# A hybrid attention and experts trunk on one core: one first-fit room for weight tiles, a three-tile split queue, a router without GpSimd

## The chip, the core and the metric

The kernel runs on one core of one Trainium2 chip. The metric is the device time of one execution in microseconds (us). TensorE multiplies, VectorE and ScalarE do elementwise work, GpSimd little of it, and SyncE (SP in the profile) issues the transfers of the weights from HBM to on-chip memory. PE is TensorE, DVE VectorE, ACT ScalarE and POOL GpSimd.

## The reference, cut to what matters

Two layers over 256 tokens of width 1024. Each layer has a norm, four kinds of attention heads side by side, an output projection and a residual add; then a norm and a SwiGLU. The first layer's SwiGLU is dense. The second's picks two of eight experts for each token:

```python
logits = (t @ router).astype(jnp.float32)
top_val, top_idx = lax.top_k(logits, TOP_K)
gates = jax.nn.softmax(top_val, axis=-1)
for e in range(N_EXPERTS):
    out = out + combine[:, e:e+1] * swiglu(t, w_gate[e], w_up[e], w_down[e])
```

An expert has matrices gate and up of 1024 x 3584 and down of 3584 x 1024, in float32. Eight experts are 352 MB of the 430 MB that the kernel reads. A final norm ends it.

## The kernel before, in words

**Weights come as a stream of tiles ("units").** `Stream` holds one ordered list for the whole kernel. Each unit is loaded in float32 by one DMA from SP's queue (L162) into a stage place. ScalarE then makes `hi`, the float16 of 512 times the weight (L169), and VectorE makes `lo`, what `hi` leaves over (L172). TensorE multiplies `hi` with the high and the low float16 part of the activations and `lo` with the high part (L1157, L1158 and L1161 for gate and up, L1190 and L1192 for down). One unit in eight of gate and up (k = 7) is left unsplit and multiplied in float32 (L1151, a flag in the unit's tuple).

**An expert is done in two halves of 1792 hidden columns.** For half i the main loop runs `gate_up(i)` and then `down(i - 1)`; `closing` does the down of the last half. A half of gate and one of up are 8 units each of 128 x 1792 (896 KB), a half of down is 7 units of two row blocks by 1024 columns (1 MB). After up, VectorE multiplies silu(gate) with up (L1178), ScalarE takes the float16 of it (L1179) and VectorE the rest (L1180). The last half's down ends in a unit of four row blocks by 512 columns and two of two row blocks by 512.

**Places.** The pool `stgp` has 9 stage buffers of 8320 bytes of a partition and `cvtp` six of 4160 for `hi` and six for `lo`, whatever the unit's size. In the last layer three more stage places are lent from elsewhere (tags e0, e2, e3, at steps 5, 10 and 16 of the attention's loop) and a fourth (xn) behind the router. A stage place is free once `lo` is made, or for an unsplit unit once TensorE has used it, and the next unit is loaded into it at once; places of `hi` and `lo` are free when TensorE has used the unit.

**Order.** The order of each engine's instructions is the order of the program. `done()` is called behind each used unit; it splits on until `ahead` units are split beyond the used one: three at the start of the kernel, then one more at every second unit up to five, and six in the experts stage. So on ScalarE and VectorE the split of a unit some places ahead stands in front of the work on a result that TensorE has yet to make. The last nine units of the list (`brisk`) are split in two parts each.

**Router.** `Plain` takes the squares of the rows (ScalarE), multiplies the rows with the norm's gain on GpSimd (`part`, L440), turns the rows on TensorE (`turn`) and multiplies them with the router matrix (`logits`). `moe` then makes the scale y of each row (`rstd_of`), the two largest logits (`top`), the one-hot masks, and the scaled rows in float16 as hh and hl. `slots(e)` makes the one-hot matrix of the slots of expert e (L1070), `gather` collects its tokens by a product with it (L1082), `gather_last` the float32 part for k = 7 (L1095, L1097). ScalarE splits one unit at the end of attention (`top_up`) and one more before the first half.

**Side work.** Gathers of the next expert and the return of the last one (`turn_back`, L1213 to L1216; `scatter`, L1222 and L1224) lie in a queue `side`. One job is taken behind each of k = 5, 6, 7 of up and behind each unit of down until the queue is empty.

Of the kernel before, what the change touches and what calls it, by code (L numbers as in the profile page):

```python
# [41 lines left out]
NB = FH // P  # L42

# [26 lines left out]
def hybrid_trunk_kernel(ctx: ExitStack, tc: tile.TileContext, a: dict, out: bass.AP, dbg=None):  # L70
# [4 lines left out]
    stgp = ctx.enter_context(tc.tile_pool(name="stgp", bufs=N_STG))  # L75
    cvtp = ctx.enter_context(tc.tile_pool(name="cvtp", bufs=N_CVT))
# [30 lines left out]
    def expert_units(sets, tail=False):  # L107

        got = []
        seq = [(s, h) for s in sets for h in range(2)]  # L110
        for i in range(len(seq) + 1):
            if i < len(seq):
                (wg, wu, _), h = seq[i]
                for w in (wg, wu):
                    got += [(rows(w, k * P, 1, h * FH, FH), 1, FH, k == KD - 1) for k in range(KD)]
            if i > 0:
                (_, _, wd), h = seq[i - 1]
                ends = tail and i == len(seq)
                got += [(rows(wd, h * FH + r * P, 2, 0, D), 2, D, False) for r in range(0, NB - 4 if ends else NB, 2)]
                if ends:  # L120
                    r0 = h * FH + (NB - 4) * P
                    got += [(rows(wd, r0 + r * P, kt, c0, 512), kt, 512, False) for r, kt, c0 in ((0, 4, 0), (0, 2, 512), (2, 2, 512))]
        return got

    MLA_KT = (2, 2, 4)
    units = []
    for layer in range(DEPTH):
# [10 lines left out]
        if layer % 2 == 0:  # L138
            units += dense_units(a["dense_w_gate"][j], a["dense_w_up"][j], a["dense_w_down"][j])
        else:  # L140
            sets = [(a["moe_w_gate"][j, e], a["moe_w_up"][j, e], a["moe_w_down"][j, e]) for e in range(NE)]
            units += expert_units(sets, layer == DEPTH - 1)

    class Stream:


        def __init__(self, units, stage_tile, part_tiles, ahead):
            self.units, self.stage_tile, self.part_tiles = units, stage_tile, part_tiles
            self.loaded = self.split = self.low = self.used = 0
            self.stage, self.place, self.high, self.ready = {}, {}, {}, {}  # L150
# [3 lines left out]
            self.brisk = 0  # L154

        def load_next(self, place=None):
            u = self.loaded
            if u < len(self.units):
                src, kt, n, _ = self.units[u]
                stg = self.stage_tile(u, place)  # L160
                self.place[u] = place
                nc.sync.dma_start(stg[:, : kt * n].rearrange("p (k n) -> p k n", k=kt), src)  # L162
                self.stage[u] = stg
                self.loaded += 1
            elif place is None and self.last:
                self.last.pop()()
# [7 lines left out]
        def split_next(self):  # L174
# [7 lines left out]
            m = self.units[u][1] * self.units[u][2]  # L182
            self.high[u] = self.part_tiles[0](u)
            self.split += 1
            if u >= len(self.units) - self.brisk:
                self.low_until(u)
                lo = self.part_tiles[1](u)
# [8 lines left out]
        def top_up(self):  # L196

            if self.split < min(len(self.units), self.used + N_CVT) and not self.units[self.split][3]:
                u = self.split
                self.high[u] = self.part_tiles[0](u)  # L200
                self.high_part(u, slice(0, self.units[u][1] * self.units[u][2]))
                self.split += 1

        def low_until(self, end):
            while self.low < end:
                if self.units[self.low][3]:
                    self.ready[self.low] = (self.stage[self.low],)
                    self.low += 1
                    continue
                lo = self.part_tiles[1](self.low)  # L210
                self.low_part(self.low, lo, slice(0, self.units[self.low][1] * self.units[self.low][2]))
                self.low_done(lo)

        def low_done(self, lo):
            u = self.low
            _, kt, n, _ = self.units[u]
            self.stage.pop(u)
            self.ready[u] = tuple(z[:, : kt * n].rearrange("p (k n) -> p k n", k=kt) for z in (self.high.pop(u), lo))
            self.low += 1
            self.load_next(self.place.pop(u))  # L220

        def get(self, later=0):
            while self.split <= self.used + later:
                self.split_next()
# [3 lines left out]
        def done(self):  # L228
# [3 lines left out]
            if self.units[u][3]:  # L232
                self.stage.pop(u)
                self.load_next(self.place.pop(u))
# [6 lines left out]
        def go(self):  # L241
            while not self.held and self.split < min(len(self.units), self.used + self.ahead):
                self.split_next()
# [10 lines left out]
    parts = (  # L254
        lambda u: cvtp.tile([P, 2080], F16, tag="hi", name=f"hi{u}"),
        lambda u: cvtp.tile([P, 2080], F16, tag="lo", name=f"lo{u}"),
    )

    def stage_tile(u, place):
        if place:  # L260
            return (ext if place[0] == "e" else com).tile([P, 2048], F32, tag=place, name=f"stg{u}")
        return stgp.tile([P, 2080], F32, tag="stg", name=f"stg{u}")

    stream = [Stream(units, stage_tile, parts, N_CVT - 1)]
    stream[0].ahead = 3
    stream[0].brisk = 9

# [158 lines left out]
    class Plain:  # L426
# [9 lines left out]
        def part(self, t, n):  # L436
# [3 lines left out]
            ge.tensor_tensor(self.xg[:, t, c], x[:, t, c], self.gain[:, c], op=OP.mult)  # L440

        def turn(self, t, half):
# [5 lines left out]
            if half == 0:  # L448
# [49 lines left out]
    def attention(layer, act, feed, follow):  # L498
# [346 lines left out]
        for i in range(NHD + 3):  # L845
# [8 lines left out]
            if i == NHD + 1 and layer == DEPTH - 1:  # L854
                late["gain"] = act.tile([P, 3, 384], F32, tag="tt", name="gain").rearrange("p a s -> p (a s)")[:, :D]
# [40 lines left out]
        wo_job("B", 1, (1,))  # L896
        nxt.part(1, 1)
        nxt.turn(1, 0)
        stream[0].top_up()
# [111 lines left out]
    def moe(layer, act, feed, follow):  # L1011
# [10 lines left out]
        feed.turn(1, 1)  # L1022
        top(0)
        pw = bank("acc", "warm_m")
        keep_warm(3, pw, ident16, cm16)
        feed.logits(1)
        ss = com.tile([P, NT], F32, tag="ss", name="ss_m")
        ve.tensor_tensor(ss, feed.ss[:, 0], feed.ss[:, 1], op=OP.add)
        y = rstd_of(ss, D, "m", NT)
# [16 lines left out]
        ve.tensor_scalar(hh[:, 1, :], xgf[:, 1, :], y[:, 1:2], None, op0=OP.mult)  # L1046
        for t in range(NT):
            se.activation(xgf[:, t, :], xgf[:, t, :], AF.Copy, scale=y[:, t : t + 1])
# [40 lines left out]
        def gather_last(e):  # L1089

            pe = pes.pop(e)
            ps = bank("side", f"gr{e}")
# [9 lines left out]
        def gathers(e):  # L1102
            return [lambda i=i, half=half: gather(e, i, half) for i in range(2) for half in range(2)] + [lambda: gather_last(e)]
# [3 lines left out]
        for t in range(NT):  # L1107
            ve.tensor_tensor(hl[:, t, :], xgf[:, t, :], hh[:, t, :], op=OP.subtract)
        ve.tensor_tensor(g2[:, :, 1], m8[:, :, 1], m8[:, :, 0], op=OP.subtract)
        ve.tensor_tensor(g2[:, :, 1], g2[:, :, 1], y, op=OP.mult)  # L1110
        se.activation(g2[:, :, 1], g2[:, :, 1], AF.Exp)
        for job in gathers(0):
            job()
# [29 lines left out]
        def into(ps, k, e):  # L1143
# [4 lines left out]
            if len(w) == 1:  # L1148
                for j in range(NB):
                    b, c = divmod(j, PER)  # L1150
                    te.matmul(ps[b][:, c * C : (c + 1) * C], w[0][:, j * P : (j + 1) * P], xr, start=False, stop=ends and j + 1 == spans[b][1])  # L1151
# [11 lines left out]

        def gate_up(i, e, tag, side):
            ps = [bank("gate", f"m{tag}g{i}_{b}") for b in range(len(spans))]
            for k in range(KD):
                into(ps, k, e)
            for b, (j0, j1) in enumerate(spans):
                se.activation(sg[:, j0 * C : j1 * C], ps[b][:, : (j1 - j0) * C], AF.Silu, scale=1.0 / SW)
            ps = [bank("up", f"m{tag}u{i}_{b}") for b in range(len(spans))]  # L1170
            for k in range(KD):
                into(ps, k, e)
                if k > 4 and side:
                    side.popleft()()
            hi, lo = hTs[i % 2]
            for b, (j0, j1) in enumerate(spans):
# [3 lines left out]
                ve.tensor_tensor(lo[:, c], sg[:, c], hi[:, c], op=OP.subtract)  # L1180

        def back_by(acc, i, r, w, k, ds):

            L = tuple(z[:, r * C : (r + 1) * C] for z in hTs[i % 2])
            first, ends = i % 2 == 0 and r == 0, i % 2 == 1 and r == NB - 1
            for part in range(2):
                for q, d in enumerate(ds):
                    dst = acc[d // 4][:, d % 4 * C : (d % 4 + 1) * C]
                    W = w[part][:, k, q * P : (q + 1) * P]
                    te.matmul(dst, W, L[0], start=first and part == 0 and d % 4 == 0, stop=ends and part == 1 and d % 4 == 3)  # L1190
                    if part == 0:
                        te.matmul(dst, W, L[1], start=False, stop=False)  # L1192

        accs = {}

        def down(i, tag, side):
            if i % 2 == 0:
                accs[i // 2] = [bank("down", f"m{tag}y{i}_{n}") for n in range(2)]
            for r in range(0, NB, 2):
# [4 lines left out]
                if side:  # L1204
                    side.popleft()()
# [27 lines left out]
        def final_gain():  # L1233
            fin["g"] = stgp.tile([P, 2080], F32, tag="stg", name="final_gain")[:, :D]
            nc.sync.dma_start(fin["g"], spread(a["final_norm"], D))
# [167 lines left out]
```

## Time and profile before

| | |
|---|---|
| median of 3 runs | 1368.21 us (1367.33 to 1368.56) |
| profiled execution | 1368.37 us, its span 1366.6 us |
| busy in the span | PE 93%, PEld (weight loads of TensorE) 83%, DVE 79%, ACT 66%, POOL 2% |
| loads of gate and up | 256 of 896 KB, 17.9 and 17.4 us to landing (median) |
| loads of down | 111 of 1 MB, 19.2 us to landing, and 2 of 512 KB |
| HBM read | 430.41 MB |

Times inside the span count from its first instruction. The router lies at 480 to 495 us, the experts behind it. In a timeline row the first number is the start and the second the duration; x is the count of instructions merged in the row, and the bracket tells how long the engine had stood idle and what ended that. "DMA share" is the mean busy share of the sixteen DMA engines (a little over 1 when all are busy), the clock a share of TensorE's full one. A matmul's own duration is its latency; matmuls overlap.

### The profile page before, as it was taken

How to read it: one execution, taken by the hardware profiler on the slowest of the kernel's cores; microseconds unless marked ns; L12 is line 12 of the kernel's file. 1: busy time of each engine (PE TensorE's matmuls, PEld its weight loads, DVE VectorE, ACT ScalarE, POOL GpSimd, SP SyncE). 2: the span in 40 equal slices, each digit the busy share in tenths (PEclk: the TensorE clock that was granted, in tenths of full speed). 3: DMA queues.
4: the chain of work that ended last, by engine and by line, in shares of the span. 5: the costliest groups of instructions: out<-in, count | busy, mean ns of one | idle time of the engine just before them, and what ended most of it. 6: DMA issues, size and time to landing. Idle time of an engine off the chain costs nothing.

```text
span 1366.6 us, 43224 instructions
## 1 busy us (share of the span) xinstructions
PE 1277.3 (93%) x19680; PEld 1134.5 (83%) x19680; DVE 1079.5 (79%) x1032; ACT 898.2 (66%) x916; POOL 32.4 (2%) x51
## 2 busy tenths in 40 slices
PE   8999999999999998999999998998998998999885
PEld 5785877777587688999989988998998998999874
DVE  6655775666564587899998898898898998989976
ACT  6554654444544576788777678677777776877764
POOL 2300000000010010000000000000000000000000
PEclk9999999999999999999999999999999999999998
DMA  9953475646443459999999999999999999999991
GB/s 272 353 171 124 155 247 198 203 149 203 156 172 111 175 196 392 400 406 414 413 411 416 412 412 416 411 411 412 408 414 402 403 416 408 410 405 407 412 361 57
DMA packets 128799, 434.35 MB, mean 318 GB/s; under 512 B 11936, under 2 KB 59440, under 8 KB 128480
## 3 DMA queue, kind: packets, MB, share of 16 engines
q1 hardware_dynamic: 126640, 429.72, 81.4%
q8 instruction: 156, 2.56, 0.8%
q0 software_dynamic: 928, 1.78, 0.5%
q14 instruction: 35, 0.29, 0.1%
q10 hardware_dynamic: 1040, 0.00, 0.0%
HBM read 430.41 MB, written 1.06 MB: 316 GB/s over the span
## 4 chain that ended last, share of the span: by engine, by line
PE 23%; DMA 19%; DVE 11%; issue 5%; ACT 3%; SPq 0%; DVEq 0%; ACTq 0%
DMA stg<-in_moe_w_down_dram 13%; DVE lo L172 8%; PE my L1190 5%; DMA stg<-in_moe_w_up_dram 3%; DMA stg<-in_moe_w_gate_dram 3%; PE mu L1151 2%; PE my L1192 2%; PE mg L1161 2%; PE mg L1158 2%; PE mg L1157 2%; PE mg L1151 1%; ACT hi L169 1%; PE mu L1158 1%; PE mu L1157 1%; PE mu L1161 1%
## 5 line engine op out<-in xcount | busy, mean ns | idle before, releaser
L172 DVE SCALAR_TENSOR_TENSOR lo<-stg,hi 128x1792 f16<-128x1792 f32 (+3 forms) x418 | 849.4, 2078 | 44.0 <-ACT hi L169 43.8
L169 ACT ACTIVATE hi<-stg 128x1792 f16<-128x1792 f32 (+3 forms) x418 | 714.4, 1738 | 154.0 <-DMA stg<-in_moe_w_down_dram 56.7
L1158 PEld LDWEIGHTS <-hi 128*128 128x128 f16 x3136 | 271.8, 98 | 11.3 <-issue 11.1
L1157 PEld LDWEIGHTS <-hi 128*128 128x128 f16 x3136 | 272.7, 99 | 4.2 <-issue 4.0
L1192 PE MATMUL my<-rest,hi 128*128 128x96 f16 x1792 | 182.9, 208 | 0.9 <-issue 0.9
L1190 PE MATMUL my<-rest,hi 128*128 128x96 f16 x1792 | 183.0, 208 | 0.3 <-issue 0.3
L1190 PEld LDWEIGHTS <-hi 128*128 128x128 f16 x1792 | 157.6, 99 | 6.2 <-issue 3.3
L1192 PEld LDWEIGHTS <-hi 128*128 128x128 f16 x1792 | 157.2, 99 | 4.1 <-issue 1.0
L1157 PE MATMUL mg<-xgh,hi 128*128 128x96 f16 x1568 | 151.3, 208 | 8.0 <-DVE x L1224 6.0
L1158 PE MATMUL mg<-xgl,hi 128*128 128x96 f16 x1568 | 151.5, 208 | 5.4 <-issue 5.3
L1161 PEld LDWEIGHTS <-lo 128*128 128x128 f16 x3136 | 146.3, 98 | 5.2 <-issue 3.5
L1157 PE MATMUL mu<-xgh,hi 128*128 128x96 f16 x1568 | 147.1, 206 | 0.1
L1158 PE MATMUL mu<-xgl,hi 128*128 128x96 f16 x1568 | 147.1, 206 | 0.0
L1190 PE MATMUL my<-rest,lo 128*128 128x96 f16 x1792 | 115.4, 208 | 7.9 <-DVE lo L172 7.2
L1190 PEld LDWEIGHTS <-lo 128*128 128x128 f16 x1792 | 89.6, 99 | 9.6 <-DVE lo L172 8.6
L1161 PE MATMUL mg<-xgh,lo 128*128 128x96 f16 x1568 | 86.7, 207 | 2.9 <-issue 2.9
L1161 PE MATMUL mu<-xgh,lo 128*128 128x96 f16 x1568 | 85.2, 206 | 0.1
L459 PEld LDWEIGHTS <-hi 128*128 128x128 f16 x640 | 62.6, 98 | 9.9 <-issue 2.7
L460 PEld LDWEIGHTS <-hi 128*128 128x128 f16 x640 | 62.6, 98 | 7.2
L461 PEld LDWEIGHTS <-lo 128*128 128x128 f16 x640 | 62.6, 98 | 7.2
L1179 ACT CAST rest<-sg 128x480 f16<-128x480 f32 (+1 forms) x48 | 27.1, 566 | 60.4 <-DVE sg L1178 60.4
L1151 PE MATMUL mu<-xr,stg 128*128 128x96 f32 x448 | 64.4, 312 | 0.0
(355 smaller groups left out, 1868.2 us busy)
## 6 DMA issues: line engine op xcount, KB each, us to landing
stg<-in_moe_w_gate_dram SPq DMA_DIRECT2D x128, 896.0 KB, 17.9
stg<-in_moe_w_up_dram SPq DMA_DIRECT2D x128, 896.0 KB, 17.4
stg<-in_moe_w_down_dram SPq DMA_DIRECT2D x111, 1024.0 KB, 19.2
stg<-in_w_in_dram SPq DMA_DIRECT2D x14, 1024.0 KB, 7.0
stg<-in_dense_w_gate_dram SPq DMA_DIRECT2D x14, 1024.0 KB, 6.5
stg<-in_dense_w_up_dram SPq DMA_DIRECT2D x14, 1024.0 KB, 5.1
stg<-in_dense_w_down_dram SPq DMA_DIRECT2D x14, 1024.0 KB, 5.0
stg<-in_w_out_dram SPq DMA_DIRECT2D x8, 1024.0 KB, 9.0
```

The lines of the kernel that those rows point to most:

```text
L169: se.activation(self.high[u][:, c], self.stage[u][:, c], AF.Copy, scale=SW)
L172: ve.scalar_tensor_tensor(lo[:, c], self.stage[u][:, c], SW, self.high[u][:, c], op0=OP.mult, op1=OP.subtract)
L459: te.matmul(ps, lh, rh, start=first, stop=False)
L460: te.matmul(ps, lh, rl, start=False, stop=False)
L461: te.matmul(ps, ll, rh, start=False, stop=last)
L1151: te.matmul(ps[b][:, c * C : (c + 1) * C], w[0][:, j * P : (j + 1) * P], xr, start=False, stop=ends and j + 1 == spans[b][1])
L1157: te.matmul(dst, L, xh[:, k, :], start=k == 0 and c == 0, stop=False)
L1158: te.matmul(dst, L, xl[:, k, :], start=False, stop=False)
L1161: te.matmul(ps[b][:, c * C : (c + 1) * C], lo[:, j * P : (j + 1) * P], xh[:, k, :], start=False, stop=ends and j + 1 == spans[b][1])
L1179: se.copy(hi[:, c], sg[:, c])
L1190: te.matmul(dst, W, L[0], start=first and part == 0 and d % 4 == 0, stop=ends and part == 1 and d % 4 == 3)
L1192: te.matmul(dst, W, L[1], start=False, stop=False)
```

## The change

- The pools for stages, `hi` and `lo` become one tile, `room`, of the same 124,800 bytes. `Room` gives places by first fit: stages from below, up to an edge, pairs of `hi` and `lo` from above it. Up to the experts the sizes and the edge are as before (9 stages, 6 pairs). From the first expert unit on each unit takes its own size (7168 or 8192 bytes, the same for its pair) and the edge stands at 11 x 7168. From the fourth half on (`lean`) the edge leaves 4 x 8192 bytes for pairs. Whenever a place is given back, loads go out as long as one fits.
- From the fourth half on three units are split ahead instead of six.
- The router: GpSimd's product goes; VectorE makes the rows times y times gain, and ScalarE copies them to float16. The row scale is made at the end of attention, as are all turns. The `top_up` there goes. The gain is loaded into the place e1 instead of the attention's tt, and ScalarE copies all turns but the first. The difference of the gates is taken behind the first gathers. The first expert's `gather_last` and the second's `slots` stand behind k = 2 of the first half's gate.
- Side jobs have fixed places: gathers behind k = 5 and 7 of up and behind the 2nd, 4th and 6th unit of down; turn-backs behind k = 5 and 6, scatters behind the 2nd to 5th unit of down. `slots` stands ahead of the half.
- The last half's down ends in five units of 512 columns: row blocks 10 and 11, then 12 and 13 of the left columns, 10 and 11, 12, and 13 of the right ones. The very last is left unsplit; for it ScalarE scales the last half's silu product by 512.

```diff
+ROOM = N_STG * 8320 + N_CVT * 8320
+EDGE = N_STG * 8320
+EDGE_X = 11 * FH * 4
+ENDS = ((0, 10, 2), (0, 12, 2), (512, 10, 2), (512, 12, 1), (512, 13, 1))
+WHOLE = ((512, 13),)
...
+        def take(self, size, below, edge):
+            for a, b in self.free if below else self.free[::-1]:
+                lo, hi = (a, min(b, edge)) if below else (max(a, edge), b)
+                if hi - lo >= size:
+                    at = lo if below else hi - size
...
+        def edge(self, u):
+            return ROOM - 4 * 8192 if self.lean else EDGE_X if u >= self.narrow else EDGE
...
+                got = places.take(self.size(u) * 4 if u >= self.narrow else 8320, True, self.edge(u))
...
+        def stage_free(self, u):
+            self.stage.pop(u)
+            place = self.place.pop(u)
+            if place or self.stage_tile:
+                self.load_next(place)
+            else:
+                places.give(self.held_by[u].pop(0))
+            while self.stage_tile is None and self.load_next():
+                pass
...
-            ge.tensor_tensor(self.xg[:, t, c], x[:, t, c], self.gain[:, c], op=OP.mult)
+
+        def rows_scale(self):
+            ss = com.tile([P, NT], F32, tag="ss", name="ss_m")
+            ve.tensor_tensor(ss, self.ss[:, 0], self.ss[:, 1], op=OP.add)
+            self.y = rstd_of(ss, D, "m", NT)
...
+        nxt.turn(1, 0)
         nxt.part(1, 1)
-        nxt.turn(1, 0)
-        stream[0].top_up()
+        nxt.turn(1, 1)
+        nxt.rows_scale()
         nxt.logits(0)
...
-        se.activation(hh[:, 0, :], xgf[:, 0, :], AF.Copy, scale=y[:, 0:1])
-        top(1)
+        for t in range(NT):
+            ve.scalar_tensor_tensor(xgf[:, t, :], x[:, t, :], y[:, t : t + 1], feed.gain, op0=OP.mult, op1=OP.mult)
+            se.copy(hh[:, t, :], xgf[:, t, :])
+            top(t)
...
+                if i == 0 and k == 2 and not tag:
+                    gather_last(0, "down")
+                    slots(1)
...
+                if i == n_half - 1 and tag == "":
+                    se.activation(sg[:, c], sg[:, c], AF.Copy, scale=SW)
...
             if i % 2 == 0 and e + 1 < NE:
-                side.append(lambda e=e: slots(e + 1))
-                side.extend(gathers(e + 1))
+                if i:
+                    slots(e + 1)
+                side.extend(zip((5, 7, 9, 11, 13), gathers(e + 1)))
             if i % 2 == 1 and e > 0:
-                side.extend(returns(e - 1))
+                side.extend(zip((5, 6, 9, 10, 11, 12), returns(e - 1)))
+            if i == 3:
+                stream[0].ahead = stream[0].most = 3
+                stream[0].lean = True
```

## Rows read from the trace of the kernel before

**Rows 1.** By stage: us; busy PE, PEld, DVE, ACT, POOL; clock, DMA share, GB/s.

```profile
497.00:545.00 48.00, 42.13 (x823) 41.73 (x821) 39.38 (x36) 34.27 (x30) 0.61 (x1) 0.93 0.98 388
545.00:600.00 55.00, 54.99 (x1155) 54.84 (x1152) 50.85 (x31) 46.76 (x34) 0.00 (x0) 1.00 1.01 397
700.00:1300.00 600.00, 553.92 (x11245) 542.39 (x11243) 542.08 (x352) 449.57 (x342) 0.00 (x0) 0.97 1.02 410
1325.00:1337.00 12.00, 12.00 (x287) 12.00 (x284) 12.00 (x12) 12.00 (x14) 0.00 (x0) 1.00 0.66 238
```

**Rows 2.** Timeline of ACT: start us, us, then the idle time before, its releaser.

```profile
705.36 1.91 ACT L169 ACTIVATE hi<-stg 128x2048 f16<-128x2048 f32 x1 [2.57 <-DMA stg<-in_moe_w_down_dram]
...
1303.17 1.91 ACT L169 ACTIVATE hi<-stg 128x2048 f16<-128x2048 f32 x1 [3.32 <-DMA stg<-in_moe_w_down_dram]
```

**Rows 3.** Line L1151, windows 560 to 610 and 610 to 660: ns, first to last.

```profile
L1151 PE MATMUL mu<-xr,stg x28: 275/275/315, 566.3 to 569.4; 128*128 128x96 f32 x28
...
L1151 PE MATMUL mu<-xr,stg x28: 274/275/315, 614.2 to 617.3; 128*128 128x96 f32 x28
```

**Rows 4.** Timeline of SP's queue: start us, us, engine, line, what, count.

```profile
478.49 0.33 SPq L162 DMA_DIRECT2D stg<-in_moe_w_up_dram  x1
...
496.98 0.33 SPq L162 DMA_DIRECT2D stg<-in_moe_w_gate_dram  x1
...
537.36 0.37 SPq L162 DMA_DIRECT2D stg<-in_moe_w_down_dram  x1
...
545.04 0.37 SPq L162 DMA_DIRECT2D stg<-in_moe_w_down_dram  x1
```

**Rows 5.** Timeline of the router, 481 to 497 us, by engine.

```profile
481.81 4.96 POOL L440 TENSOR_TENSOR xg<-x,gain 128x512 f32<-128x512 f32 x4 [9.71 <-PE wo L461]
...
481.71 0.69 DVE L736 SCALAR_TENSOR_TENSOR x<-wo,x 128x512 f32<-128x512 f32 x1 [0.60 <-PE wo L461]
...
485.61 1.20 DVE L357 TENSOR_SCALAR v_m<-ss_m 128x2 f32<-128x2 f32 x1
...
487.70 0.16 DVE L362 SCALAR_TENSOR_TENSOR y_m<-z_m,y_m 128x2 f32<-128x2 f32 x1
...
488.69 0.17 DVE L1045 TENSOR_TENSOR mk<-oh 128x16 f16<-128x16 f32 x1
...
483.59 1.70 ACT L169 ACTIVATE hi<-stg 128x1792 f16<-128x1792 f32 x1
...
495.35 1.70 ACT L169 ACTIVATE hi<-stg 128x1792 f16<-128x1792 f32 x1
...
495.03 0.24 PE L1157 MATMUL mg<-xgh,hi 128*128 128x96 f16 x1
```

**Rows 6.** Timeline between the first two halves, PE and DVE.

```profile
535.41 0.24 PE L1157 MATMUL mg<-xgh,hi 128*128 128x96 f16 x1 [1.82 <-DVE xgl L1087]
...
524.82 0.44 DVE L1070 TENSOR_SCALAR back<-cm,share 128x96 f16<-128x96 f32 x2
...
535.28 2.02 DVE L172 SCALAR_TENSOR_TENSOR lo<-stg,hi 128x1792 f16<-128x1792 f32 x1
...
542.99 9.77 DVE L172 SCALAR_TENSOR_TENSOR lo<-stg,hi 128x1792 f16<-128x1792 f32 x5 [1.34 <-ACT hi L169]
```

**Rows 7.** Groups of instructions, 497 to 1337 us: busy, mean ns, idle before.

```profile
L1082 PE MATMUL gx<-back,hh_m 128*128 128x96 f16 x112 | 9.1, 231 | 25.9 <-DVE back L1070 25.9
```

**Rows 8.** The tail: timeline of DVE, then forms, 1303 to 1348.

```profile
1335.81 11.57 DVE L172 SCALAR_TENSOR_TENSOR lo<-stg,hi 128x1024 f16<-128x1024 f32 x12
...
L172 DVE SCALAR_TENSOR_TENSOR lo<-stg,hi 128x1024 f16<-128x1024 f32 x14 | 16.2, 1218 | 0.0
L172 DVE SCALAR_TENSOR_TENSOR lo<-stg,hi 128x2048 f16<-128x2048 f32 x6 | 13.7, 2286 | 3.7 <-ACT hi L169 3.7
...
L172 DVE SCALAR_TENSOR_TENSOR lo<-stg,hi 128x512 f16<-128x512 f32 x4 | 2.5, 686 | 0.0
...
L1151 PE MATMUL mu<-xr,stg 128*128 128x96 f32 x28 | 3.3, 274 | 0.0
```

More of the change, by code (lines that the diff above doesn't have):

```diff
@@ new lines, in part_tile @@
+        def part_tile(self, u, low):
+            size = self.size(u) * 2 if u >= self.narrow else 4160
+            if not low:
+                pair = places.take(2 * size, False, self.edge(u))
+                both = [(pair[0], size), (pair[0] + size, size)] if pair else [places.take(size, False, self.edge(u)) for _ in range(2)]
+                if not all(both):
+                    for got in filter(None, both):
+                        places.give(got)
+                    return None
+                self.held_by.setdefault(u, []).extend(both)
+            return at(self.held_by[u][low - 2], F16)
@@ L232, in done @@
             if self.units[u][3]:
-                self.stage.pop(u)
-                self.load_next(self.place.pop(u))
+                self.stage_free(u)
+            else:
+                for got in self.held_by.pop(u):
+                    places.give(got)
             if self.later:
@@ L1102, in gathers @@
         def gathers(e):
-            return [lambda i=i, half=half: gather(e, i, half) for i in range(2) for half in range(2)] + [lambda: gather_last(e)]
+            last = [lambda: gather_last(e)] if e else []
+            return [lambda i=i, half=half: gather(e, i, half) for i in range(2) for half in range(2)] + last
         keep_warm(2, pw, ident16, cm16)
@@ L1162, in into, with beside @@
             unit_done()
+        def beside(side, at):
+            while side and side[0][0] <= at:
+                side.popleft()[1]()
         def gate_up(i, e, tag, side):
@@ L1172, in gate_up @@
                 into(ps, k, e)
-                if k > 4 and side:
-                    side.popleft()()
+                beside(side, k)
             hi, lo = hTs[i % 2]
@@ L1203, in down @@
                 unit_done()
-                if side:
-                    side.popleft()()
+                beside(side, KD + r // 2)
         def finish(acc, n):
@@ L1233, in final_gain @@
         def final_gain():
-            fin["g"] = stgp.tile([P, 2080], F32, tag="stg", name="final_gain")[:, :D]
-            nc.sync.dma_start(fin["g"], spread(a["final_norm"], D))
+            got = places.take(D * 4, True, EDGE_X)
+            if got:
+                fin["g"] = at(got, F32)
+                nc.sync.dma_start(fin["g"], spread(a["final_norm"], D))
+            return got
         stream[0].last.append(final_gain)
@@ L1337, in moe @@
             else:
-                while side:
-                    side.popleft()()
+                beside(side, 99)
             assert not side
```

166 lines of the change are left out of this document (98 added, 68 removed).

## The prediction

> **What bounds the kernel now.** I read the busy time of each engine by stage first [rows 1]. From 700 to 1300 us the sixteen DMA engines are busy in a share of 1.02 and move 410 GB/s: the experts stage runs at the speed of its weights. VectorE is 90% busy there (542.08 of 600 us) and TensorE 92%, so both have a little room and no more. Between 497 and 600 us the share is 0.98 and 1.01 but the rate only 388 and 397 GB/s. After 1325 us the transfers run out while VectorE stays at 12.00 of 12 us: the end hangs on VectorE.
>
> Two paces follow. ScalarE's hi of the first tile of down waits for its landing at 705.36 and again, eleven halves of an expert later, at 1303.17 [rows 2]: 597.8 / 11 = 54.4 us a half, which is the DMA's pace. Early, while tiles lay ready, the eighth product of up began at 566.3 and again at 614.2 [rows 3]: the engines alone need 47.9 us a half with splits up to six tiles ahead. They have a backlog at the start and have worked it off by 705, where they wait for landings.
>
> So the time is: the moment from which the DMA never rests again, plus fixed bytes at a fixed rate, plus VectorE's work behind the landing of the last half but one's first tile of down, plus a fixed close. An edit counts only where it moves one of these.
>
> **One room.** A gate or up tile takes 7168 bytes of a partition, not 8320. Before, 9 + 3 places hold tiles before the router ends; the last load before it is issued at 478.49 and none follows until 496.98 [rows 4]. By then 16 expert tiles were issued (four had been split). By the first-fit rule, followed tile by tile, the room holds 11 of 7168 bytes below EDGE_X, so 18 are issued. Two tiles of 896 KB (0.92 MB) at 410 GB/s are a lead of 4.5 us.
>
> **Router without GpSimd.** GpSimd's four products run from 481.81 for 4.96 us, and VectorE's product on 128x2 takes 1.20 us and ends as they do [rows 5]; another of that size takes 0.16. Without them y is ready about 485.1, not 487.86 (487.70 + 0.16). But the two products with the gain are now VectorE's and stand ahead of the top-2: at 0.69 us for 512 columns (the closest row, the residual add of L736) about 1.25 us for each 1024, 2.5 in all, so the mask is ready at about 489.0, against 488.69 + 0.17 = 488.86. Then the exponential of the gates no longer stands ahead of the gather's copies on ScalarE, and the last gather moves into the first products. I take the first product at 494.1 instead of 495.03: a gain of 0.9, between 0 and 2.5. Against it, the fifth tile's hi is no longer made at 483.59 in a hole of the router, but behind the gates at about 495.3 (where the sixth stood, 495.35). Its lo ends at about 499.1, and loads wait for that lo: the DMA starts 2.1 us after 496.98. The lead is 4.5 - 2.1 = 2.4 us.
>
> **What becomes of the lead.** Between the first half and the second, VectorE turns to the silu product, the shares and the gathered tokens; TensorE stands until 535.41, the 35th tile is issued at 537.36, the 37th at 545.04 [rows 4, 6]. Here the number of places decides, and the room has no more of them: tiles of down need 8192 bytes, which fit no hole of 7168, so by the same rule 35 are issued before the wait, the 36th behind the lo that ends at 535.28 + 2.02 = 537.30, the 37th behind the first lo of the row from 542.99 as before, and the 38th one lo (9.77 / 5 = 1.95 us) later than before. The lead is spent as rest between 535 and 545; after that the queue is never empty in either kernel. At that pass VectorE saves the 0.44 us of the slots, made earlier now, and TensorE is some 0.2 earlier: -0.6 us. The later 38th costs +1.1 once it has queued. In 545 to 600 the queue is a tile or so deeper; the stretch loses 55 x (1 - 397/410) = 1.7 us, of which I give back half. Together -0.6 + 1.1 - 0.9 = -0.4 us, and between -4.9 (nothing of the lead is spent, the other gains stay) and +3.
>
> **Fixed places for side work.** TensorE's wait for the slots (L1070), 25.9 us in all, goes, since they are made before the half; but it is idle time of an engine that is not the bound [rows 7]. Gathers at k 5 and 7 and beside down, scatters one tile later: nothing. Cover: the DMA's 54.4 us. If it were gone, TensorE's own 9.1 us of gathers on that line would show.
>
> **Shorter queue.** From the fourth half on only three tiles are split ahead and 12 places of 7168 bytes hold loads. More loads in flight buy nothing at a share of 1.02. What the short queue does is couple the engines: hi of tile u+3 takes the place that TensorE leaves with tile u, and the DMA's slack of 54.4 - 47.9 = 6.5 us a half has to cover that. From hi's 1.70 and lo's 1.95 us [rows 5, 6] I estimate up to 1.6 us where a tile is used unsplit (two in a half: the hi behind it waits for TensorE instead of running ahead), 1.1 behind the first of these, and nothing else: at most 4.3 of the 6.5. So it costs nothing in the steady part, though VectorE comes to the tail with a lag of 0 to 2.8 us; I take 0.5.
>
> **The tail.** The first tile of down of the last half but one has landed at 1303.17, where ScalarE's hi starts on it [rows 2]. VectorE's last lo ends at 1335.81 + 11.57 = 1347.38 [rows 8], 44.2 us behind the landing. Its lo's sum to 6 x 2.286 + 14 x 1.218 + 4 x 0.686 = 33.5 us. Afterwards: eight whole ones 18.3, eight halves 9.7, six halves of 512 columns 4.1, and two of 256 columns, bounded by 0.16 (128x2) and 0.69 (512) and taken as 0.4 each, midway: 32.9. Less by 0.6. The turn-back's two subtractions now stand ahead of the first lo and push its start by 0.5; the unsplit tile adds four float32 products behind the last lo, 4 x 3.3/28 = 0.5 us; lag 0.5. Tail: -0.6 + 0.5 + 0.5 + 0.5 = +0.9 us, between -0.6 (only the splits count) and +3.2 (the lag at its most). From the last lo to the end, 1366.6 - 1347.4 = 19.2 us, the rest is as before. Three more copies of sg on ScalarE lie beside VectorE's steps, as do two more issues.
>
> **Other edits.** The gain goes to e1 and is fetched earlier; nothing waited for it. Turns copied by ScalarE instead of VectorE: within the router's sum.
>
> **Sum.** -0.4 + 0.9 = +0.5 us. The profiled execution took 1368.37 (span 1366.6 and 1.77 around it), 0.16 above the median shown. **1368.9 us**, no difference that can be told; 0.2%, 2.7 us, is about what can.
>
> **Rivals.** *Faster: the lead lives.* If the room holds one or two tiles more at the pass than I count, or the engines get through the pass sooner, DMA rests less there: up to -4.5 of places and -1 of pass, with the tail as worked out, 1368.9 - 5 = about 1364 us. For it: the queue before is dry exactly there (537.36 to 545.04). Against: places of 8192. Chance 0.30. The Trainium skill ("Perfetto Trace Analysis", Optimization Strategy) says that a gap repeating on the engine that should be saturated can mean too little on-chip memory for the next tile. By it, more places would shorten every half; the rows give it this one pass and not the halves from 700 us, where the DMA has no gap.
>
> *Slower: the short queue becomes the bound.* Place: from the fourth half, VectorE and TensorE in lockstep, with TensorE standing while VectorE is in the silu block and its clock falling afterwards (mean 0.97 in 700 to 1300). It decides once a half of the engines takes over 54.4 us, that is if the coupling costs over 6.5. At 55.2 it is 13 halves x 0.8 = 10 us; short of that, a backlog not worked off comes to the tail. 1368.9 + 7 = about 1376 us. Chance 0.33. For it: VectorE's 90%. Against: my 4.3.
>
> *The room doesn't do what it says*: it is one tile, and if a load waited for all its readers, the DMA would rest in each half, over 20 us slower. Against: `back` is already cut up among three engines without such waits. Chance 0.02.
>
> **Numbers.** No change 0.35, faster 0.30, slower 0.35. The forecast's own range is 1366 to 1371, the bounds of its terms without the lead, cut where the difference could be told. For 8 in 10 it reaches to the lead with a short tail, 1361, and to the short queue at 13 x 0.8, 1379.
>
> **What would show it.** In the changed profile: 18 tiles issued before the router ends and the next load near 499; DMA at rest around 535 to 545; from 700 on 410 GB/s at about 54.4 us a half, VectorE waiting for landings; last lo some 44 to 46 us behind the landing of the last half but one's first tile of down; about 19 us from there to the end. Wrong would be: no dip at 540, which gives the first rival; hi's or lo's that wait for TensorE in most halves while GB/s falls below 405, which gives the second; a last lo under 42 us behind that landing.

## The result and the profile after

The changed kernel takes 1375.89 us (median of 19 runs, 1369.74 to 1378.00), the kernel before 1368.18 in the same sittings (19 runs, 1366.28 to 1369.99): a ratio of 1.0051, 95% interval 1.0042 to 1.0060. It is slower by 7.7 us by the medians (7.0 by the ratio), where the forecast was no change at 1368.9. The profiled execution is one of the quicker ones: 1372.92 us, its span 1371.1, 4.5 us over that of before; the first readings below account for these 4.5, and those of two slower executions for the rest.

By stage, as in [rows 1]:

```profile
497.00:545.00 48.00, 42.75 (x866) 42.45 (x864) 43.07 (x37) 36.11 (x33) 0.57 (x1) 0.93 0.91 359
545.00:600.00 55.00, 53.93 (x1123) 53.61 (x1120) 48.72 (x31) 45.29 (x33) 0.00 (x0) 1.00 0.97 394
700.00:1300.00 600.00, 554.29 (x11133) 542.24 (x11132) 540.59 (x348) 453.21 (x345) 0.00 (x0) 0.96 1.02 410
1325.00:1337.00 12.00, 12.00 (x207) 10.97 (x205) 12.00 (x9) 8.78 (x7) 0.00 (x0) 0.80 0.52 196
```

From 700 to 1300 us nothing in this row betrays a loss: the transfers move 410 GB/s at a share of 1.02, as before. What changed there is who waits for whom. In the changed kernel a stage, hi and lo all bear the name room: an ACT row room<-room or room<-stg is a hi, such a DVE row a lo. PE rows of mg and mu are the products of gate and up, those of my the products of down. ScalarE's waits in that stretch, the changed kernel first (us in total, times, longest), then the kernel before:

```profile
ACT room L249 <- PE my L1286: 24.3, 41, 1.5
ACT room L249 <- PE mu L1240: 23.9, 23, 1.7
ACT room L249 <- PE mg L1240: 23.4, 17, 2.6
ACT room L249 <- PE my L1284: 17.4, 11, 2.0
ACT room L249 <- PE mu L1243: 7.7, 11, 1.0
...
ACT room L249 <- DMA room<-in_moe_w_down_dram: 1.9, 1, 1.9
```

```profile
ACT hi L169 <- DMA stg<-in_moe_w_down_dram: 51.3, 57, 3.3
...
ACT hi L169 <- DMA stg<-in_moe_w_up_dram: 31.1, 46, 2.1
```

Before, hi waited 82 us for landings and 14 for TensorE. After, it waits 97 us in the five rows for TensorE to leave a place, and two or three us for a landing. The tiles have long landed. The first tile of down of the fourth half, and that of the last half but one, whose landing was the anchor of the prediction [rows 2], show it. SP's queue, the median from issue to landing in the windows 691 to 692 and 1282 to 1284 us (which hold these issues alone), and ScalarE's hi on the two tiles:

```profile
691.45 0.38 SPq L220 DMA_DIRECT2D room<-in_moe_w_down_dram  x1
...
1283.51 4.50 SPq L220 DMA_DIRECT2D room<-in_moe_w_down_dram  x3
```

```profile
room<-in_moe_w_down_dram SPq DMA_DIRECT2D x1, 1024.0 KB, 11.9
...
room<-in_moe_w_down_dram SPq DMA_DIRECT2D x1, 1024.0 KB, 16.8
```

```profile
713.13 1.91 ACT L249 ACTIVATE room<-room 128x2048 f16<-128x2048 f32 x1 [1.70 <-PE mu L1240]
...
1307.85 1.91 ACT L249 ACTIVATE room<-room 128x2048 f16<-128x2048 f32 x1 [1.70 <-PE mu L1240]
```

The later one lands at 1283.51 + 16.8 = 1300.3, that is 2.9 us earlier than the 1303.17 of before, and ScalarE takes it up 7.5 us after landing. The engines are behind the transfers in every half alike: the same idle 1.70 us with the same releaser stands ahead of the first tile of down in all twelve halves from 713.13 to 1307.85. At 713.13 the tile had landed at 691.45 + 11.9 = 703.4, 9.8 us before. Worked out in the same way the lag lies between 7.5 and 10.6 us at all twelve tiles: it comes out of the early halves and is not worked off, where the kernel before waited for the landing at 705.36 already [rows 2]. At the end VectorE closes as follows:

```profile
1342.28 8.90 DVE L252 SCALAR_TENSOR_TENSOR room<-room 128x1024 f16<-128x1024 f32 x12
1352.60 0.69 DVE L1310 TENSOR_TENSOR back<-yte,back 96x512 f16<-96x512 f32 x1 [1.41 <-ACT back L1309]
```

The last lo ends at 1351.18, 50.9 us behind that landing instead of 44.2 [rows 8], and the close takes 1371.1 - 1351.2 = 19.9 us instead of 19.2. So -2.9 + 6.7 + 0.7 = +4.5 us: in this execution the transfers gained 2.9, the engines' lag took 6.7.

Two kernels below that take the changed kernel's time, with the edge left (profiled execution 1376.47 us) and with the old cut of the last tiles (1375.47), show the usual loss. The same tile with the edge left:

```profile
1290.99 0.38 SPq L220 DMA_DIRECT2D room<-in_moe_w_down_dram  x1
```

```profile
room<-in_moe_w_down_dram SPq DMA_DIRECT2D x1, 1024.0 KB, 12.2
```

```profile
1311.80 1.91 ACT L249 ACTIVATE room<-room 128x2048 f16<-128x2048 f32 x1 [1.70 <-PE mu L1240]
```

It lands at 1303.2, as before, and is taken up 8.6 us later; with the old cut it lands at 1286.82 + 16.0 = 1302.8 and is taken up at 1310.90, 8.1 us later. From landing to the last lo it takes 51.8 and 51.7 us instead of 44.2, 7.6 and 7.5 more, where the spans are 8.0 and 7.0 longer than that of before. There the transfers gain next to nothing, and the lag is about all of the loss. Why they were 2.9 us ahead in the quicker execution stays open.

### The profile page after: what moved, and what is told of

The parts are those of the page before. It is cut to its first block, busy times and chain, and to the rows that moved or that the text cites. A ratio compares the mean times of both kernels' runs of the same rounds, so it can differ in the third digit from the quotient of the medians.

```text
span 1371.1 us, 43203 instructions
## 1 busy us (share of the span) xinstructions
PE 1282.8 (94%) x19673; PEld 1137.9 (83%) x19673; DVE 1080.5 (79%) x1032; ACT 898.3 (66%) x919; POOL 27.4 (2%) x47
## 3 DMA queue, kind: packets, MB, share of 16 engines
HBM read 430.41 MB, written 1.06 MB: 315 GB/s over the span
## 4 chain that ended last, share of the span: by engine, by line
PE 41%; DVE 10%; DMA 4%; ACT 4%; issue 2%; SPq 0%; DVEq 0%; ACTq 0%
PE my L1284 9%; DVE room L252 6%; PE mg L1243 4%; PE my L1286 4%; PE mg L1240 4%; PE mg L1239 4%; PE mu L1240 4%; PE mu L1239 3%; PE mu L1243 3%; PE mg L1233 3%; DMA room<-in_moe_w_gate_dram 2%; ACT room L249 2%; ACT rest L1268 2%; DVE sg L1267 1%; DVE rest L1269 1%
## 5 line engine op out<-in xcount | busy, mean ns | idle before, releaser
L252 DVE SCALAR_TENSOR_TENSOR room<-room 128x1792 f16<-128x1792 f32 (+6 forms) x320 | 652.6, 2069 | 80.8 <-ACT room L249 78.1
L249 ACT ACTIVATE room<-room 128x1792 f16<-128x1792 f32 (+6 forms) x320 | 548.6, 1734 | 235.0 <-issue 61.2
L1284 PE MATMUL my<-rest,room 128*128 128x96 f16 x3576 | 261.3, 214 | 50.3 <-DVE room L252 50.2
L1284 PEld LDWEIGHTS <-room 128*128 128x128 f16 x3576 | 249.5, 103 | 57.7 <-DVE room L252 52.5
L1240 PEld LDWEIGHTS <-room 128*128 128x128 f16 x3136 | 270.4, 98 | 7.0 <-issue 6.6
L1239 PEld LDWEIGHTS <-room 128*128 128x128 f16 x3136 | 271.1, 98 | 4.5 <-issue 4.1
L252 DVE SCALAR_TENSOR_TENSOR room<-stg,room 128x1792 f16<-128x1792 f32 (+2 forms) x98 | 203.9, 2096 | 8.9 <-ACT room L249 8.5
L249 ACT ACTIVATE room<-stg 128x1792 f16<-128x1792 f32 (+2 forms) x98 | 170.6, 1755 | 36.5 <-PE mg L1240 12.4
L1286 PE MATMUL my<-rest,room 128*128 128x96 f16 x1788 | 193.1, 214 | 0.2 <-issue 0.2
L1286 PEld LDWEIGHTS <-room 128*128 128x128 f16 x1788 | 165.6, 103 | 4.3 <-issue 1.7
L1239 PE MATMUL mg<-xgh,room 128*128 128x96 f16 x1568 | 149.5, 207 | 7.6 <-ACT peT L1181 4.4
L1240 PE MATMUL mg<-xgl,room 128*128 128x96 f16 x1568 | 149.4, 207 | 2.1 <-issue 2.0
L1243 PEld LDWEIGHTS <-room 128*128 128x128 f16 x3136 | 145.8, 98 | 5.7 <-issue 2.1
L1240 PE MATMUL mu<-xgl,room 128*128 128x96 f16 x1568 | 147.0, 206 | 0.3 <-issue 0.3
L1239 PE MATMUL mu<-xgh,room 128*128 128x96 f16 x1568 | 146.9, 206 | 0.0
L1243 PE MATMUL mg<-xgh,room 128*128 128x96 f16 x1568 | 86.3, 207 | 1.7 <-issue 0.9
L1243 PE MATMUL mu<-xgh,room 128*128 128x96 f16 x1568 | 85.4, 206 | 0.2 <-issue 0.2
L545 PEld LDWEIGHTS <-room 128*128 128x128 f16 x640 | 62.9, 98 | 10.1 <-issue 2.7
L546 PEld LDWEIGHTS <-room 128*128 128x128 f16 x640 | 62.9, 98 | 7.5
L547 PEld LDWEIGHTS <-room 128*128 128x128 f16 x640 | 62.9, 98 | 7.5
```

Source lines behind the costliest of these rows:

```text
L249: se.activation(self.high[u][:, c], self.stage[u][:, c], AF.Copy, scale=SW)
L252: ve.scalar_tensor_tensor(lo[:, c], self.stage[u][:, c], SW, self.high[u][:, c], op0=OP.mult, op1=OP.subtract)
L545: te.matmul(ps, lh, rh, start=first, stop=False)
L546: te.matmul(ps, lh, rl, start=False, stop=False)
L547: te.matmul(ps, ll, rh, start=False, stop=last)
L1239: te.matmul(dst, L, xh[:, k, :], start=k == 0 and c == 0, stop=False)
```

## The experiments

The theories, as the expectations name them: **S**, the short queue lets the engines come late to the end; **T**, the new cut of the last tiles; **F**, the front (router, first fit). Later **P**, the choice of the place; **Q**, too few places; **L**, a lead is spent between 540 and 550 us. The three kernels with shortened loads ran once each; of the others there are 11 runs beside the kernel before, where no other count stands.

**One part at a time.** The kernel before with the short queue alone:

```diff
+            if i == 3:
+                stream[0].ahead = stream[0].most = 3
             if i < n_half:
```

> The kernel before with one edit: from the fourth half on three units are split ahead instead of six (its pools keep 9 + 4 stage places and six pairs). Theory S (the short queue lets the engines come to the last half about 6 us behind the transfers): 5 to 8 us slower than before, a ratio of 1.004 to 1.006, last hi's before the end waiting for TensorE and no longer for landings, still 410 GB/s from 700 to 1300 us. Theory T (the new cutting of the last tiles costs the time) and theory F (the new router and the room's first fit cost it): no change, 0.999 to 1.001.

Measured: 1366.87 us, a ratio of 0.9989 (0.9980 to 0.9998). Not slower by 5 to 8 us as S had it; if anything faster by 1.5 us. S in this form falls: three units ahead cost no time where the places are the old ones, six of hi and six of lo. The changed kernel without the short queue:

```diff
-            if i == 3:
-                stream[0].ahead = stream[0].most = 3
-                stream[0].lean = True
```

> The changed kernel without the short queue: six units ahead and the lower edge of the room to the end, all else as changed. Theory S: the 6 us of lag go and the lead of about 1.4 us that the transfers have at 700 us is left, so 1366 to 1369 us, a ratio of 0.998 to 1.001 to before; hi's of down wait for landings again. Theories T and F: as slow as the changed kernel, a ratio near 1.005.

Measured: 1368.75 us, 1.0001 (0.9992 to 1.0010). The loss is gone, as S had it; neither T nor F can hold it. The two runs together say that the short queue costs only in company with another part of the change, of which the room is the one that deals with places. The old cut of the last tiles in the changed kernel:

```diff
-ENDS = ((0, 10, 2), (0, 12, 2), (512, 10, 2), (512, 12, 1), (512, 13, 1))
-WHOLE = ((512, 13),)
+ENDS = ((0, 10, 4), (512, 10, 2), (512, 12, 2))
+WHOLE = ()
...
-                if i == n_half - 1 and tag == "":
-                    se.activation(sg[:, c], sg[:, c], AF.Copy, scale=SW)
```

> The changed kernel with the last half's down cut as before (four row blocks by 512, then two of two by 512, all split, no scaled copy). Theory T: the time of before, a ratio of 0.998 to 1.001. Theories S and F: within 1 us of the changed kernel, a ratio of 1.004 to 1.006; the prediction's own sum gives the cut 0.1 us.

Measured: 1375.43 us (5 runs), 1.0048 (1.0034 to 1.0061). T falls. Then the short queue only up to the fourteenth half:

```diff
+            if i == 13:
+                stream[0].ahead = stream[0].most = 6
+                stream[0].lean = False
```

> The changed kernel, but from the fourteenth half (of sixteen) on six units are split ahead again and the room's edge is the lower one. Theory S, in the form that the short queue costs nothing but the lag it leaves at the end: two to three halves with some 6 us of slack each work the lag off, so the time is that of the changed kernel with six throughout, a ratio of 0.998 to 1.001. If the short queue costs something in each half of the steady part, most of the 7 us stay: 1.003 to 1.005. Theories T and F: 1.005.

Measured: 1366.85 us, 0.9992 (0.9983 to 1.0001). Ten halves with the short queue cost nothing that lasts: three halves with six ahead pay all of it back. What costs is the lag that is left at the end.

**Which property of the room.** `lean` raises the edge so that four pairs are left. When a unit is used and the third next asks for its pair, two of the four are held and two are free: the one that TensorE is just leaving and one that it left earlier. `take` searches from the top. The first run leaves the edge where it was (five or six pairs), the second keeps four pairs but gives them out in turn:

```diff
             if i == 3:
                 stream[0].ahead = stream[0].most = 3
-                stream[0].lean = True
```

> The changed kernel with three units ahead from the fourth half, but without the raised edge (five or six pairs of places as in the halves before it). Theory P (first fit from the top gives hi the place that TensorE is just leaving, however many lie free below it, so that ScalarE waits for TensorE): as slow as the changed kernel, 1374 to 1377 us. Theory Q (four pairs are too few for three units ahead): the time of the kernel with six throughout or of the short queue alone, 1366 to 1369 us.

```diff
...
-                pair = places.take(2 * size, False, self.edge(u))
+                pair = None
+                if self.lean:
+                    pair = places.take_at(ROOM - 8192 * (1 + self.turn % 4), 2 * size)
+                    self.turn += 1
+                pair = pair or places.take(2 * size, False, self.edge(u))
```

> The changed kernel with all of it, four pairs and three units ahead, but from the fourth half on each pair is put into the next of the four places in turn, so that hi of a unit takes a place that was left one unit earlier. Theory P: the waits of ScalarE for TensorE mostly go and those for landings come back; 1365 to 1368 us, since the transfers' lead of about 1.4 us is left. Theory Q: four pairs remain, 1374 to 1377 us.

Measured: with the edge left, 1376.75 us (6 runs), 1.0059 (1.0042 to 1.0075); in turn, 1365.85 us, 0.9983 (0.9974 to 0.9992). More places don't help, the same four in another order do: P holds and Q falls. First fit from the top gives the next hi the pair that TensorE is just leaving, since that is the topmost free one, while a free pair lies below it unused. Followed step by step through `take` and `give` for the 189 split tiles of nine halves, from the fifth on, 171 are given the pair of the tile just used, whether the edge is raised or left, and with places in turn none; no pair fails to fit in any of the three, so holes of the wrong size are not the reason. With six ahead in the room it is 168 of 189 as well, at the time of before: the place costs only where few split tiles lie between. ScalarE's waits, 700 to 1300 us, with the edge left:

```profile
ACT room L249 <- PE mg L1240: 29.1, 22, 2.6
ACT room L249 <- PE mu L1240: 23.5, 21, 2.2
ACT room L249 <- PE my L1286: 19.4, 32, 1.8
ACT room L249 <- PE my L1284: 17.0, 11, 2.0
```

and with the places in turn, where the first tile of down is again taken up as it lands (room's waits for TensorE come to 21 us there, and the lag is gone from the tile on that lands at 976.0):

```profile
ACT room L263 <- PE my L1300: 16.1, 25, 1.3
...
ACT room L263 <- DMA room<-in_moe_w_down_dram: 13.3, 8, 3.1
ACT room L263 <- DMA room<-in_moe_w_up_dram: 11.7, 12, 2.7
```

```profile
1301.37 1.91 ACT L263 ACTIVATE room<-room 128x2048 f16<-128x2048 f32 x1 [3.01 <-DMA room<-in_moe_w_down_dram]
```

**The engines' own half.** Three kernels in which the transfers are no longer the bound, since most loads leave out half of their columns:

```diff
+            dst = stg[:, : kt * n].rearrange("p (k n) -> p k n", k=kt)
+            if place is None and self.narrow and u >= self.narrow + 177:
+                dst, src = dst[:, :, : n // 2], src[:, :, : n // 2]
-            nc.sync.dma_start(stg[:, : kt * n].rearrange("p (k n) -> p k n", k=kt), src)
+            nc.sync.dma_start(dst, src)
```

> The changed kernel, but from the ninth half on a load into the room moves only the first half of its columns (loads into the four lent places are whole), so the rest of such a tile is what lay there before; each engine has the same instructions. It shows the engines' own half with the short queue, the transfers no longer the bound. Theory P: 54 to 55 us from one eighth product of up to the next, which is the transfers' old pace, so that a lag cannot be worked off; my estimate ahead of the result: at most 47.9 + 4.3 = 52.2 us.

> The same shortened loads in the changed kernel without the short queue and the raised edge. All theories: 47 to 49 us a half, as the halves that had tiles ready took in the kernel before; the difference to the run with the short queue is what the places cost the engines per half: 6 to 7 us by theory P, at most 4.3 by my estimate.

> The shortened loads from the ninth half on with the four places in turn. The engines' own half: 54.0 us with the pair on top (measured with the same loads), 51.4 with six ahead. Theory P: 50 to 52 us, that is two or more below the pair on top. If the wait for TensorE's place is not what costs, 54.

The eighth product of up, at the tenth half and at the last, six halves later, and the stage between, in this order: pair on top; six ahead; four in turn.

```profile
L1236 PE MATMUL mu<-xr,stg x28: 248/275/275, 985.8 to 988.8; 128*128 128x96 f32 x28
...
L1236 PE MATMUL mu<-xr,room x22: 248/275/275, 1309.6 to 1311.9; 128*128 128x96 f32 x22
...
980.00:1300.00 320.00, 294.18 (x5938) 287.65 (x5936) 289.11 (x187) 240.64 (x181) 0.00 (x0) 0.96 0.77 262
```

```profile
L1236 PE MATMUL mu<-xr,stg x28: 248/275/275, 978.3 to 981.3; 128*128 128x96 f32 x28
L1236 PE MATMUL mu<-xr,stg x28: 248/275/275, 1286.6 to 1289.6; 128*128 128x96 f32 x28
```

```profile
L1250 PE MATMUL mu<-xr,stg x28: 248/275/275, 981.5 to 984.5; 128*128 128x96 f32 x28
...
L1250 PE MATMUL mu<-xr,room x28: 248/275/275, 1297.1 to 1300.1; 128*128 128x96 f32 x28
```

(1309.6 - 985.8) / 6 = 54.0 us a half with the pair on top, 51.4 with six ahead, 52.6 with four in turn. From 980 to 1300 us a hi or lo waits 2.5 us in all for landings with six ahead, and not at all in the other two, so these are the engines' paces. With the pair on top the run took 1371.29 us in all: at a DMA share of 0.77 and 262 GB/s the time is still among those of the changed kernel (1369.74 to 1378.00). So that kernel runs at its engines' pace, which happens to be that of the transfers (54.4), and a lag once there stays. The other two took 1344.55 and 1358.11. The pair on top is as theory P had it (54 to 55, against my own 52.2 at most). Missed were six ahead at 47 to 49, a difference of 6 to 7, where it is 2.6, and four in turn at 50 to 52, two or more below the pair on top, where it is 1.4 below. So by one run of each the choice of the place is 1.4 of the 2.6 us, and 1.2 stay with three units ahead in turn. With these 1.2 a half of the engines is still 1.8 us shorter than one of the transfers, and a lag can be worked off. What the 1.2 are is not shown; a wait that the short queue brings in either order is TensorE's for the lo of the first tiles of down, 497 to 1337 us, here in the changed kernel, with places in turn and before:

```profile
PE my L1284 <- DVE room L252: 50.2, 14, 4.2
```

```profile
PE my L1298 <- DVE room L266: 43.2, 18, 5.0
```

```profile
PE my L1190 <- DVE lo L172: 6.9, 7, 4.1
```

**What the rest is worth once the lag is gone.** All three start from the four places in turn. First, the old cut of the last tiles, as in the diff above:

> The kernel with the four places in turn, and the last half's down cut as before. It shows what the new cut is worth where the engines are not late (the run in turn: a ratio of 0.9983 to before). My sum: the cut saves 0.6 us of splits and costs 0.5 for the unsplit products, so the same within 1 us, 0.998 to 0.999. If the cut is worth more than its splits (its last units are smaller, so the end hangs on less), 1.000 or above.

Measured: 1365.42 us, 0.9980 (0.9971 to 0.9989): the same. Second, a fifth hi ahead of the router:

```diff
         nxt.rows_scale()
+        stream[0].top_up()
```

> The kernel with the four places in turn, with a fifth hi put back at the end of attention, ahead of the router's copies, so that its lo and the next load come about 2 us earlier. Theory L (a lead won in the router is spent as rest of the transfers between 540 and 550 us, where no place is free): the DMA share there falls further by some 2 us, and the time is the same, 0.998 to 0.999. If the lead lives: 2 us less, 0.9965 to 0.997. If the hi ahead of the router's copies holds up the first product: up to 1.7 us more.

Measured: 1365.75 us, 0.9988 (0.9979 to 0.9997): the same. The stages, with four in turn, then with the hi put back:

```profile
497.00:515.00 18.00, 18.00 (x358) 18.00 (x356) 16.95 (x11) 16.78 (x16) 0.00 (x0) 0.94 0.82 314
530.00:540.00 10.00, 5.16 (x66) 4.96 (x64) 7.21 (x15) 3.49 (x6) 0.57 (x1) 0.66 1.03 403
540.00:550.00 10.00, 10.00 (x239) 10.00 (x236) 7.72 (x5) 7.13 (x5) 0.00 (x0) 1.00 0.65 230
```

```profile
497.00:515.00 18.00, 18.00 (x382) 18.00 (x379) 15.98 (x11) 15.89 (x15) 0.00 (x0) 1.00 0.97 373
530.00:540.00 10.00, 5.78 (x104) 5.67 (x104) 7.53 (x14) 4.37 (x6) 0.57 (x1) 0.83 0.94 356
540.00:550.00 10.00, 10.00 (x212) 10.00 (x210) 8.29 (x6) 7.80 (x6) 0.00 (x0) 1.00 0.51 184
```

18 x (373 - 314) = 1.06 MB more by 515, 2.6 us at 410 GB/s; 10 x (47 + 46) = 0.93 MB, 2.3 us, less from 530 to 550. L holds. Third, five places and four ahead:

```diff
-            return ROOM - 4 * 8192 if self.lean else EDGE_X if u >= self.narrow else EDGE
+            return ROOM - 5 * 8192 if self.lean else EDGE_X if u >= self.narrow else EDGE
...
-                    pair = places.take_at(ROOM - 8192 * (1 + self.turn % 4), 2 * size)
+                    pair = places.take_at(ROOM - 8192 * (1 + self.turn % 5), 2 * size)
...
-                stream[0].ahead = stream[0].most = 3
+                stream[0].ahead = stream[0].most = 4
```

> Five places in turn and four units ahead, one place less for loads. Theory P with the transfers as the bound from there on: the same as four in turn, 0.998 to 0.999. If the engines with four places are still close to the bound and lag now and then, up to 1 us less; if the loads miss their place, over 1.000 and under 409 GB/s from 700 to 1300 us.

Measured: 1365.84 us, 0.9989 (0.9980 to 0.9998): the same. The kernels with places in turn beat both kernels: by the ratios 1.5 to 2.7 us the one before, over 8 us the changed one.

## Where the prediction failed and where it held, point by point

The measured 1375.89 us lies above the forecast's own range, 1366 to 1371, and inside the wide one, 1361 to 1379, which reaches so far because of the second rival.

**The step that failed: "the DMA's slack of 54.4 - 47.9 = 6.5 us a half has to cover that".** 47.9 came from two starts of one early half [rows 3] and was taken for all. That half has no turn-back or scatter of an earlier expert, which begin with the fourth. The prediction's own rows spoke against it: from 700 to 1300 us VectorE alone is busy 542.08 / 600 x 54.4 = 49.1 us a half [rows 1]. By the shortened loads the engines need 51.4 us on the mean of six halves with six ahead in the room, so the slack is 3.0. The coupling itself I had at most at 4.3 us; it is 54.0 - 51.4 = 2.6, inside the bound. But 2.6 of 3.0 is all but everything, and of the lag of 9.8 us at the fourth half's tile 7.5 are left eleven halves later. From this followed the mis-sized term: "VectorE comes to the tail with a lag of 0 to 2.8 us; I take 0.5". Landing to last lo is 6.7 us longer, where the sum had -0.6 + 0.5 + 0.5 = 0.4; from there to the end it is 0.7 longer, where the sum had 0.5.

**The mechanism was named, its remedy not seen.** "hi of tile u+3 takes the place that TensorE leaves with tile u" is what the waits show. I took it as given by the queue's length. The place is given by the search from the top: with the same queue hi waits for TensorE 21 us from 700 to 1300 us with places in turn, and under 2 with the old pools, instead of 97.

**The second rival** came true in its milder half, "a backlog not worked off comes to the tail", and its 1376 us is the time measured. That the size fits too is luck in part: its 7 us were chosen between 0 and 10, not worked out. Its sign, GB/s below 405, did not come: the transfers moved 410 though the engines took the tiles up 7 to 10 us after landing.

**One room and the lead**: right in kind. Between 380 and 490 us 17 expert tiles are issued where 15 were, and the next load comes at 499.5 (499 foretold). The transfers do rest at the pass, 236 GB/s from 540 to 545 and 209 from 545 to 550, against 306 and 349 before. What is left I put at -0.4 us in bounds of -4.9 to +3; the landing at 1300.3 makes it -2.9 in the profiled execution, but those at 1302.8 and 1303.2, in the executions with the old cut and with the edge left, -0.4 and 0. The first rival, *the lead lives*, has at most the 2.9 of the truth. That a further lead is spent, the run with the fifth hi shows.

**Router**: no gain shown. y is ready at 486.14, not 485.1, and the mask at 490.11, not 489.0, since the attention's last residual add ends 1.3 us later in this execution (483.05 + 0.69 against 481.71 + 0.69 in [rows 5]); the first product starts at 495.38 (495.03 before). The products with the gain take 1.28 and 1.27 us (1.25 foretold).

```profile
483.05 0.69 DVE L822 SCALAR_TENSOR_TENSOR x<-wo,x 128x512 f32<-128x512 f32 x1 [0.85 <-PE wo L547]
...
485.98 0.16 DVE L444 SCALAR_TENSOR_TENSOR y_m<-z_m,y_m 128x2 f32<-128x2 f32 x1
486.18 1.28 DVE L1115 SCALAR_TENSOR_TENSOR xg<-x,y_m,gain 128x1024 f32<-128x1024 f32 x1
487.74 1.27 DVE L1115 SCALAR_TENSOR_TENSOR xg<-x,y_m,gain 128x1024 f32<-128x1024 f32 x1
489.94 0.17 DVE L1129 TENSOR_TENSOR mk<-oh 128x16 f16<-128x16 f32 x1
...
495.38 0.20 PE L1239 MATMUL mg<-xgh,room 128*128 128x96 f16 x1 [0.77 <-DVE xgl L1168]
```

Across runs the first product spreads: 493.86 to 496.40 with the new router, 495.03 and 496.16 with the old one. A gain or loss under 1 us can't be told from these.

**Fixed side work**: right. TensorE's 25.9 us of waiting for the slots [rows 7] are gone, and with six ahead, where the fixed places are too, the time is that of before (1.0001):

```profile
L1163 PE MATMUL gx<-back,hh_m 128*128 128x96 f16 x112 | 7.0, 206 | 0.0
```

**The cut of the tail**: right. The two lo's of 256 columns were taken as 0.4 us each and took 0.41; the old cut gives the same time with the lag and without it.

The Trainium skill ("Perfetto Trace Analysis", Optimization Strategy) says that a gap which repeats along the engine that should be saturated can mean that memory for the next tile is short, in count or size of buffers. Here the gap of 1.70 us repeats on ScalarE, 66% busy, and with more places it stands as it was, at 1311.80 with the edge left: not their count but which of the free ones is taken decided.

## What to carry to other kernels

Where an allocator gives out the place freed last, a short queue can become a wait for the reader that is just leaving it, as here; give places out in turn, so that the one freed longest ago is taken. A DMA share of 1.02 didn't say here that the engines kept up: look whether the engine that first reads a landed tile (here ScalarE, for hi) waits for landings or for places, and compare a tile's landing with the start of its first use. To know the engines' own pace, shorten the loads and count several periods, not one; and check it against the busy time of each engine per period, which it can't undercut.

## What the runs showed that was not expected

The short queue with the old pools is not merely free: landing to last lo is 43.2 us there, and 43.0 with places in turn, against 44.2. Only three hi's stand ahead of the last silu block instead of six, so TensorE gets the first tiles of down sooner. That this is the cause of the 1.5 to 2 us was argued from the order, not tried by itself.

The changed kernel's 19 runs spread over 8.3 us, the 6 with the edge left over 7.0, but the 5 with the old cut over 2.6 only. The 19 of before spread over 3.7, the 11 of the kernel with four places in turn over 2.0 (1365.23 to 1367.21), those of its three variants over 2.4 to 4.2. So two of the three kernels at their engines' pace repeat less closely than those that wait for landings; why stays open.
